# A two-layer decoder trunk in three-product fp32: pairs of hidden blocks from a feed-forward's first block on, the first pair's products in another order, and room handed back sooner

## The chip, the cores and the metric

The kernel runs on one core of a Trainium2 chip. The metric is device microseconds of one execution, the median of several. One row of a profile is one instruction (or a group of like ones) with its start and duration on an engine: PE is the matrix engine, DVE the vector engine, ACT the scalar engine, POOL the GpSimd engine, SP the one that issues most DMAs.

## The reference, cut to what matters

Two layers, each a half-step feed-forward, a mixer (attention and a state-space scan), and a second half-step feed-forward, over 512 tokens of width 1024. The change touches the feed-forwards (FFN) and the hand-over from the mixer to the second one.

```python
def rms_norm(x, gain):
    return x * lax.rsqrt(jnp.mean(x * x, axis=-1, keepdims=True) + NORM_EPS) * gain

def swiglu(h, w_up, w_down):
    gate, up = jnp.split(h @ w_up, 2, axis=-1)          # 1024 -> 2 * 2816
    return (jax.nn.silu(gate) * up) @ w_down            # 2816 -> 1024

for l in range(2):
    x = x + 0.5 * swiglu(rms_norm(x, ffn1_norm[l]), ffn1_w_up[l], ffn1_w_down[l])
    x = x + mixer(rms_norm(x, mix_norm[l])) @ w_out[l]
    x = x + 0.5 * swiglu(rms_norm(x, ffn2_norm[l]), ffn2_w_up[l], ffn2_w_down[l])
return rms_norm(x, final_norm)
```

## The kernel before

Activations lie feature-major: eight tiles `x[m]` of 128 features by 512 tokens. Every product in full precision is three matmuls on rounded operands (`mm3`): high part times high part (L292), high activation times low weight (L293), low activation times high weight (L294). So each activation tile is split into `hhi` (ACT, L477) and `hlo` (DVE, L479), and each weight unit into `whi` (ACT, L259) and `wlo` (DVE, L261).

A weight unit is 128 x 1024 numbers (512 KB): `fetch` issues its load on SP (L219), `convert` splits it, both some units ahead of use. `unit_order` writes the order of all units out; PE uses them in just that order. Everything but the matmuls and the loads runs as small generators, stepped by `tick` while PE's matmuls are written: a `yield n` puts a step n ticks later, and `spawn(g, n)` starts one n ticks late. The instruction order of each engine follows from that; each engine then works through its own queue in order.

An FFN has 22 hidden blocks of 128 in three slices (0-7, 8-15, 16-21); after each slice come eight `down` units, one for each output tile `m`. A hidden block in the ordinary way is a gate unit and an up unit of 24 matmuls over 512 tokens each. Two blocks (j and j+1) can instead be done as a "pair" (`pair_of_blocks`): seven products in the manner of Strassen, in the order of `SEVEN`, with 24 matmuls over 256 tokens each. The products named 11, 12, s2, s1, s3, s4, 22 use four stored weight units and three sums. The weight sums are made here: s1 and s3 by a load on SP (L225) and an accumulating DMA on POOL's queue (L231, in `onto`), s2 = s1 + unit 11 and then s4 = s2 + unit 12 by DVE additions (L244, in `add`). Products 11, 12 and s4 read the split tiles `h`; s2, s1, s3 and 22 read combined inputs `diff`, four pairs of tiles `th` (ACT, L364) and `tl` (DVE, L368), which `combine` makes from `x` (`uv`, L352 to L359) once for each FFN. `combine` starts when an `x` tile is final (from `x_final`), or by fixed delays in the first FFN of layer 0.

Which blocks go as pairs is told by `pairs_from`: in the first FFN of layer 0 blocks 6 to 21, in the other three blocks 2 to 21. The norm's factor `rs` comes late: matmuls run on gain-scaled inputs, and `rs` is multiplied into gate and up (DVE L523; POOL L536; in pairs L599). `FFN (layer, f)` below counts f as 1 and 2. In each FFN but the first, the last steps of the part before it (`down` or `out` units) finish the eight `x` tiles one by one: x (L625 or L1094), `hhi`, `hlo`, the square (`sq`, `acc`, L496) and `combine`.

Of the kernel before, what the change touches and what calls it, by code (L numbers as in the profile page):

```python
# [11 lines left out]
ALU = mybir.AluOpType  # L12
# [4 lines left out]
P = 128  # L17
SEQ = 512
# [15 lines left out]
SEVEN = ("11", "12", "s2", "s1", "s3", "s4", "22")  # L34
STORED = ("11", "12", "s1", "22")
# [105 lines left out]
class Builder:  # L141
# [7 lines left out]
    def __init__(self, ctx, tc, xT, wflat, par, taps, out):  # L149
# [10 lines left out]
        self.sums, self.early, self.summed = {}, {}, 0  # L160
# [53 lines left out]
    def fetch(self, i):  # L214
# [8 lines left out]
        for key in self.early.get(i, ()):  # L223
            raw = self.t(self.sx, [P, KB * P], key[-1], bufs=2)
            self.nc.sync.dma_start(raw, self.stored(key[:-1] + ("s1",)))  # L225
            self.spawn(self.onto(key, raw), 9)
# [20 lines left out]
    def convert(self, i):  # L247
# [7 lines left out]
        elif key[-1] in ("s2", "s4"):  # L255
            raw = self.sums[key[:-1] + ("s2",)]
# [7 lines left out]
    def ahead(self, look=LOOK):  # L264
# [80 lines left out]
    def combine(self, k, gain):  # L345
# [4 lines left out]
        x = self.x[k]  # L350
# [3 lines left out]
        yield 2  # L354
# [5 lines left out]
        yield 1  # L360
        two = []
        for t in (u, v):
            two.append(self.t(self.tp, [P, SEQ], "th", F32R, bufs=KB))
            nc.scalar.copy(two[-1], t)  # L364
            yield 2
        for i, t, hi in zip((k, m), (u, v), two):
# [3 lines left out]
            yield 1  # L370
# [178 lines left out]
    def pair_of_blocks(self, base, fp, two):  # L549
# [5 lines left out]
        lower, upper = self.h[:n], self.h[n:]  # L555
# [47 lines left out]
        product(chain, "11", lower, a, True)  # L603
        nc.scalar.copy(g1, chain)
        product(ps2, "12", upper, a, True)
# [7 lines left out]
        nc.scalar.copy(c, ps3)  # L613
        product(chain, "s3", diff[:n], b, False)
        nc.vector.tensor_tensor(c, chain, c, op=ALU.add)
        self.spawn(normed_up(c))
        product(ps3, "s4", upper, b, False)
        nc.vector.tensor_tensor(g2, g2, ps3, op=ALU.add)
        self.spawn(activate(g2, up2, b))
# [9 lines left out]
    def x_final(self, m, gain):  # L629
        x = self.x[m]  # L630
        yield 1
        if gain is not None:
            yield from self.norm_split(m, gain)
            if self.tp is not None and m >= KB // 2:
                self.spawn(self.combine(m - KB // 2, gain), 2)
# [461 lines left out]
    def mixer(self, layer):  # L1097
# [13 lines left out]
        with ExitStack() as mix:  # L1111
# [6 lines left out]
            gp = enter(tc.tile_pool(name=f"gates{layer}", bufs=2, reuse_waits="tile"))  # L1118
# [42 lines left out]
            with tc.tile_pool(name=f"mg{layer}", bufs=KB, reuse_waits="tile") as mg, \  # L1161
                    tc.tile_pool(name=f"gr{layer}", bufs=2, reuse_waits="tile") as gr:
# [25 lines left out]
                branches.close()  # L1188
                self.open_x()
                self.open_t()  # L1190
                for m in OUT_ORDER:
                    nc.sync.dma_start(self.x[m], xd[m])
                    ps = self.t(self.pmm, [P, SEQ], "mm")
                    self.dense(ps, self.unit(layer, "out", m), self.merged, 0, KB)
                    if m == 0:
                        self.norm_start()
                    self.spawn(self.mix_out(ps, m, gain))
# [164 lines left out]
```

## Time and profile before

| | |
|---|---|
| median of 3 runs | 2616.57 us (2616.45 to 2617.44) |
| profiled execution | 2617.7 us, span 2615.8 us |
| granted PE clock | 0.998 |
| PE busy | 2592.5 us, 99% |
| DVE busy | 1750.1 us, 67% |
| ACT / POOL busy | 1299.0 us, 50% / 508.9 us, 19% |
| chain that ended last | PE 93%, DVE 4%, ACT 1%, DMA 1% |

Where the four FFNs start ordinary blocks and pairs in this execution (us from the span's start): in FFN (0,1) block 4 starts at 52.72 and the first pair at 76.36; FFN (0,2) starts at 961.73 and its first pair at 984.40; FFN (1,1) at 1305.74 and 1330.21; FFN (1,2) at 2256.06 and 2278.73. A busy share is the union of an engine's instruction times over the span. Matmuls overlap in the records, so that their pitch (start to start) and not their duration is what one costs.

### The profile page before, as it was taken

Reading aid. Unit: us, or ns where it says so; the run is one execution under the profiler, and the core shown is the slowest. Engines: PE = TensorE matmul, PEld = TensorE weight load, DVE = VectorE, ACT = ScalarE, POOL = GpSimd, SP = SyncE. Lnnn points to the kernel's source line nnn. Section 1 sums busy time; section 2 is a strip of 40 time slices with the busy share of each in tenths; the row PEclk is TensorE's granted clock in tenths of the full one; section 3 lists DMA queues with packets and bytes.
Section 4 is the critical chain, followed back from the end, with each engine's and each line's share of the span. In section 5 each row is a group of like instructions: output and inputs, shape, how many; then the busy total and the mean of one; then the engine's idle time right before and its main releaser. Section 6 shows DMA issues by size and latency. Waiting matters only on the chain.

```text
span 2615.8 us, 38022 instructions
## 1 busy us (share of the span) xinstructions
PE 2592.5 (99%) x15000; PEld 2289.3 (88%) x15000; DVE 1750.1 (67%) x2352; ACT 1299.0 (50%) x2094; POOL 508.9 (19%) x629
## 2 busy tenths in 40 slices
PE   9999999999999999999999999999999999999997
PEld 7898988888888889899998989888888888899996
DVE  7576876565665478585885858766666744776765
ACT  6343556655554255353553535566555543543444
POOL 1121201133232003021120312012332410121110
PEclk9999999999999999999999999999999999999999
DMA  6555442333323546463554644423333235474642
GB/s 182 141 150 140 122 138 76 104 107 106 114 91 99 163 145 163 136 184 110 159 144 123 179 127 131 130 79 105 98 117 105 97 105 155 138 183 129 177 120 75
DMA packets 102850, 336.35 MB, mean 129 GB/s; under 512 B 12000, under 2 KB 13280, under 8 KB 102672
## 3 DMA queue, kind: packets, MB, share of 16 engines
q1 hardware_dynamic: 91440, 294.00, 35.7%
q0 software_dynamic: 10944, 39.85, 8.7%
q8 instruction: 118, 1.93, 0.3%
q14 instruction: 60, 0.49, 0.1%
q10 hardware_dynamic: 288, 0.07, 0.0%
HBM read 321.20 MB, written 12.68 MB: 128 GB/s over the span
## 4 chain that ended last, share of the span: by engine, by line
PE 93%; DVE 4%; ACT 1%; DMA 1%; issue 1%; POOL 0%; SPq 0%; DVEq 0%; ACTq 0%
PE mm L292 26%; PE mm L294 26%; PE mm L293 26%; PE pa L293 3%; PE pa L294 3%; PE pa L292 3%; PE pa L999 1%; PE pt L762 1%; PE pa L836 1%; DVE wlo L261 1%; PE pa L1001 1%; PE pt L984 1%; PE pt L982 1%; DVE cv L900 0%; ACT whi L259 0%
## 5 line engine op out<-in xcount | busy, mean ns | idle before, releaser
L259 ACT CAST whi<-wraw 128x1024 fp32r<-128x1024 f32 (+2 forms) x434 | 434.2, 1000 | 592.2 <-PE mm L294 504.6
L292 PE MATMUL mm<-hhi,whi 128*128 128x512 f32 (+1 forms) x1856 | 679.5, 366 | 1.1 <-ACT hhi L477 1.1
L293 PE MATMUL mm<-hhi,wlo 128*128 128x512 f32 (+1 forms) x1856 | 658.8, 355 | 2.3 <-DVE wlo L261 2.1
L294 PE MATMUL mm<-hlo,whi 128*128 128x512 f32 (+1 forms) x1856 | 660.4, 356 | 0.1
L261 DVE TENSOR_TENSOR wlo<-wraw,whi 128x1024 fp32r<-128x1024 f32 (+2 forms) x434 | 542.3, 1250 | 168.2 <-ACT whi L259 166.3
L294 PEld LDWEIGHTS mm<-hlo,whi 128*128 128x128 f32 x1856 | 350.9, 189 | 51.7 <-DVE hlo L479 0.5
L293 PEld LDWEIGHTS mm<-hhi,wlo 128*128 128x128 f32 x1856 | 351.7, 190 | 47.1 <-DVE wlo L261 3.5
L292 PEld LDWEIGHTS mm<-hhi,whi 128*128 128x128 f32 x1856 | 351.5, 189 | 44.0 <-ACT hhi L477 1.5
L599 POOL TENSOR_TENSOR g<-g,rs 128x512 f32<-128x512 f32 x76 | 133.2, 1752 | 735.8 <-DVE g L606 715.3
L261 DVE TENSOR_TENSOR wlo<-s,whi 128x1024 fp32r<-128x1024 f32 x152 | 235.5, 1563 | 58.2 <-ACT whi L259 58.2
L292 PE MATMUL mm<-act,whi 128*128 128x512 f32 x704 | 274.0, 389 | 0.0
L293 PE MATMUL mm<-act,wlo 128*128 128x512 f32 x704 | 274.0, 389 | 0.0
L294 PE MATMUL mm<-act,whi 128*128 128x512 f32 x704 | 273.9, 389 | 0.0
L292 PE MATMUL mm<-th,whi 128*128 128x256 f32 x912 | 258.1, 283 | 0.0
L293 PE MATMUL mm<-th,wlo 128*128 128x256 f32 x912 | 258.1, 283 | 0.0
L294 PE MATMUL mm<-tl,whi 128*128 128x256 f32 x912 | 258.1, 283 | 0.0
L259 ACT CAST whi<-s 128x1024 fp32r<-128x1024 f32 x152 | 158.9, 1046 | 100.5 <-PE mm L294 59.0
L625 DVE SCALAR_TENSOR_TENSOR x<-mm,x 128x512 f32<-128x512 f32 x96 | 66.1, 689 | 201.1 <-PE mm L294 201.1
L292 PEld LDWEIGHTS mm<-th,whi 128*128 128x128 f32 x912 | 175.1, 192 | 0.0
L293 PEld LDWEIGHTS mm<-th,wlo 128*128 128x128 f32 x912 | 175.1, 192 | 0.0
L294 PEld LDWEIGHTS mm<-tl,whi 128*128 128x128 f32 x912 | 175.1, 192 | 0.0
L900 DVE SCALAR_TENSOR_TENSOR cv<-mm,conv,cv 128x511 f32<-128x511 f32 (+2 forms) x192 | 142.4, 742 | 24.7 <-ACT cv L897 22.8
(256 smaller groups left out, 4538.7 us busy)
## 6 DMA issues: line engine op xcount, KB each, us to landing
wraw<-in_wflat_dram SPq DMA_DIRECT2D x354, 512.0 KB, 3.7
s<-in_wflat_dram SPq DMA_DIRECT2D x76, 512.0 KB, 5.5
s<-in_wflat_dram POOLq DMA_DIRECT2D x76, 512.0 KB, 9.3
wraw<-in_wflat_dram SPq DMA_DIRECT2D x64, 384.0 KB, 3.1
cumb<-cum_d SPq DMA_DIRECT2D x16, 768.0 KB, 4.0
xd<-x SPq DMA_DIRECT2D x16, 256.0 KB, 3.2
wraw<-in_wflat_dram SPq DMA_DIRECT2D x16, 256.0 KB, 3.2
x<-xd SPq DMA_DIRECT2D x16, 256.0 KB, 5.3
```

The source lines that it names most:

```text
L259: nc.scalar.copy(hi[:, :n], raw[:, :n])
L261: nc.vector.tensor_tensor(lo[:, :n], raw[:, :n], hi[:, :n].bitcast(F32), op=ALU.subtract)
L292: mm(ps, a[0], b[0], start=start, stop=False, **kw)
L293: mm(ps, a[1], b[0], start=False, stop=False, **kw)
L294: mm(ps, a[0], b[1], start=False, stop=stop, **kw)
L599: eng.tensor_tensor(r, r, self.rs[:, cols].unsqueeze(1).to_broadcast([P, 2, half]), op=ALU.mult)
L625: self.nc.vector.scalar_tensor_tensor(x, pd, 0.5, x, op0=ALU.mult, op1=ALU.add)
L762: self.nc.tensor.transpose(pt[:, cs], src[:, cs], self.ident)
L836: nc.tensor.matmul(pz[:, (i - j) * P:n], lhs, part, start=False, stop=(i == j and part is sps[i][1]), skip_group_check=True)
L900: nc.vector.scalar_tensor_tensor(u[:, i:], ps[:, :SEQ - i], tap[KCONV - 1 - i], u[:, i:], op0=ALU.mult, op1=ALU.add)
L982: nc.tensor.matmul(pc[:, :P], bt[:, span(c)], ct[:, span(c)], start=True, stop=True)
L984: nc.tensor.matmul(pu, btok[:, c, :], xws[c].rearrange("p h d -> p (h d)"), start=True, stop=True)
```

## The change

Four pairs take the place of eight ordinary blocks: pairs begin at block 4 in FFN (0,1) and at block 0 in the other three. Since the combined inputs are then wanted at once, the first pair of each FFN runs its products in the order 11, 12, s4, s2, s1, s3, 22 (`FIRST_SEVEN`), where the first three read `h` alone. For that s4 gets a tile and a PSUM bank of its own, and its addition comes before the other's use. The tiles of s1 to s4 move to the pool of the combined inputs, which is open from the mixer on, so the loads of s1 and s3 are no longer held to the FFN's fifth unit: s1 is loaded with the unit two before 11, s3 with 11. `combine` takes other delays. In the mixer the gate tiles go to the side of the branch pools and are closed with them, after the first `out` unit, and the eight loads of `x` are then issued together.

```diff
+FIRST_SEVEN = ("11", "12", "s4", "s2", "s1", "s3", "22")
 def pairs_from(layer, f):
-    return 6 if (layer, f) == (0, 1) else 2
+    return 4 if (layer, f) == (0, 1) else 0
 # unit_order
-                    for part in SEVEN:
+                    for part in (FIRST_SEVEN if j == pairs_from(layer, f) else SEVEN):
 # the weight stream's set-up
-            if key[2:] == ("gate", 0):
-                first = i + 4
-            if "pair" in key and key[-1] in ("s1", "s3"):
-                self.early.setdefault(max(first, i - (5 if key[-1] == "s1" else 4)), []).append(key)
+            if "pair" in key and key[-1] == "11":
+                self.early[i - 2], self.early[i] = key[:-1] + ("s1",), key[:-1] + ("s3",)
 # fetch
-            raw = self.t(self.sx, [P, KB * P], key[-1], bufs=2)
+            raw = self.t(self.tp, [P, KB * P], key[-1], bufs=2)
 # add
-            r = a = self.sums[base + ("s2",)]
-            b = self.sums.pop(base + ("12",))
+            yield 3
+            a, b = self.sums[base + ("s2",)], self.sums.pop(base + ("12",))
+        r = self.sums[key] = self.t(self.tp, [P, KB * P], key[-1], bufs=1)
 # ahead
-            if self.keys[i][-1] in ("s2", "s4"):
-                self.spawn(self.add(self.keys[i]))
+            key = self.keys[i]
+            if key[-1] in ("s2", "s4") and key not in self.adding:
+                for part in (("s2", "s4") if self.keys[i - 1][-1] == "12" and key[-1] == "s4" else key[-1:]):
+                    self.adding.add(key[:-1] + (part,))
+                    self.spawn(self.add(key[:-1] + (part,)))
 # combine
+        x, pause = self.x[k], 1 if m == KB - 1 else 2
...
         two = []
         for t in (u, v):
+            yield pause
             two.append(self.t(self.tp, [P, SEQ], "th", F32R, bufs=KB))
             nc.scalar.copy(two[-1], t)
-            yield 2
+        yield pause
         for i, t, hi in zip((k, m), (u, v), two):
             lo = self.t(self.tp, [P, SEQ], "tl", F32R, bufs=KB)
             nc.vector.tensor_tensor(lo, t, hi.bitcast(F32), op=ALU.subtract)
             self.diff[i] = (hi, lo)
-            yield 1
 # pair_of_blocks
+        first = base[-1] == pairs_from(*base[:2])
+        if first:
+            ps4 = self.t(self.pa, [P, SEQ], "pa")
+            product(ps4, "s4", self.h[n:], b, True)
         product(chain, "s2", diff[n:], b, False)
         nc.scalar.copy(g2, chain)
+        if first:
+            nc.vector.tensor_tensor(g2, g2, ps4, op=ALU.add)
...
 # ffn
-                            self.spawn(self.combine(k, gain), 10 + 9 * k)
+                            self.spawn(self.combine(k, gain), 10 + 8 * k)
 # mixer: the last projection
-                branches.close()
-                self.open_x()
-                self.open_t()
                 for m in OUT_ORDER:
-                    nc.sync.dma_start(self.x[m], xd[m])
                     ps = self.t(self.pmm, [P, SEQ], "mm")
                     self.dense(ps, self.unit(layer, "out", m), self.merged, 0, KB)
                     if m == 0:
+                        branches.close()
+                        self.open_x()
+                        self.open_t()
+                        for r in OUT_ORDER:
+                            nc.sync.dma_start(self.x[r], xd[r])
                         self.norm_start()
-                    self.spawn(self.mix_out(ps, m, gain))
+                    self.spawn(self.mix_out(ps, m, gain), 9 if m == 0 else 0)
```

What this does to the queues is seen at three places. The names in the rows carry instance numbers; `s` is a weight sum, `mm` and `pa` are PSUM banks, `a` and `act` the product silu(gate) * up and its split.

The first place is DVE around block 4 of FFN (0,1). Before, these rows prepare the gate and up units of blocks 4 and 5:

```order
L261 TENSOR_TENSOR wlo_514<-wraw_385,whi_513 128x1024
L368 TENSOR_TENSOR tl_530<-uv_476,th_500 128x512
L368 TENSOR_TENSOR tl_535<-uv_477,th_519 128x512
L355 SCALAR_TENSOR_TENSOR uv_537<-x_89,par_106,uv_537 128x256
L356 TENSOR_TENSOR uv_537<-uv_538,uv_537 128x256
L358 SCALAR_TENSOR_TENSOR uv_538<-uv_537,uv_538 128x256
L359 SCALAR_TENSOR_TENSOR uv_538<-uv_538 128x256
L523 TENSOR_TENSOR g_502<-mm_503,rs_390 128x512
L261 TENSOR_TENSOR wlo_565<-wraw_445,whi_564 128x1024
```

Now the first `wlo` below is that of product 11, the second that of 12, the third that of s4, the fourth that of s2:

```order
L261 TENSOR_TENSOR wlo_515<-wraw_383,whi_514 128x1024
L361 SCALAR_TENSOR_TENSOR uv_521<-uv_520,uv_521 128x256
L362 SCALAR_TENSOR_TENSOR uv_521<-uv_521 128x256
L371 TENSOR_TENSOR tl_554<-uv_520,th_544 128x512
L371 TENSOR_TENSOR tl_556<-uv_521,th_549 128x512
L525 TENSOR_TENSOR g_505<-mm_506,rs_390 128x512
L244 TENSOR_TENSOR s_116_569<-s_57_288,wraw_383 128x1024
L261 TENSOR_TENSOR wlo_567<-wraw_447,whi_566 128x1024
L244 TENSOR_TENSOR s_117_582<-s_116_569,wraw_447 128x1024
L547 TENSOR_TENSOR a_610<-mm_561,g_505 128x512
L387 TENSOR_TENSOR act_380<-a_610,act_379 128x512
L261 TENSOR_TENSOR wlo_613<-s_117_582,whi_612 128x1024
```

Between the first and the second weight split of the place stand now the last two `tl` steps and the addition of s2, and before the third the addition of s4; both are wanted by PE half as long apart as before, since a pair's product has matmuls of half the length.

The second place is POOL's queue at the very start. Before:

```order
L454 AFFINE_SELECT tri<-neg 128x128
L536 TENSOR_TENSOR g_169<-g_169,rs_390 128x512
L536 TENSOR_TENSOR g_285<-g_285,rs_390 128x512
L536 TENSOR_TENSOR g_383<-g_383,rs_390 128x512
L231 DMA s_100_506<-in_wflat_dram 128x1024
L536 TENSOR_TENSOR g_502<-g_502,rs_390 128x512
```

Now:

```order
L456 AFFINE_SELECT tri<-neg 128x128
L231 DMA s_57_288<-in_wflat_dram 128x1024
L538 TENSOR_TENSOR g_166<-g_166,rs_390 128x512
L538 TENSOR_TENSOR g_282<-g_282,rs_390 128x512
L231 DMA s_75_385<-in_wflat_dram 128x1024
L538 TENSOR_TENSOR g_381<-g_381,rs_390 128x512
```

The first accumulating DMA (of s1) moved from behind three multiplications by `rs` to the head of the queue, the second (s3) to behind two of them.

The third place is DVE at the start of FFN (1,1), where the last two `x` tiles (m = 3 and 7) are finished. Before:

```order
L625 SCALAR_TENSOR_TENSOR x_8555<-mm_12238,x_8555 128x512
L358 SCALAR_TENSOR_TENSOR uv_12273<-uv_12272,uv_12273 128x256
L359 SCALAR_TENSOR_TENSOR uv_12273<-uv_12273 128x256
L479 SCALAR_TENSOR_TENSOR hlo_12297<-x_8555,par_107,hhi_12296 128x512
L261 TENSOR_TENSOR wlo_12289<-wraw_12198,whi_12288 128x1024
L496 TENSOR_TENSOR acc_12081<-acc_12081,sq_12305 128x512
L368 TENSOR_TENSOR tl_12345<-uv_12272,th_12302 128x512
L625 SCALAR_TENSOR_TENSOR x_8559<-mm_12279,x_8559 128x512
L368 TENSOR_TENSOR tl_12354<-uv_12273,th_12315 128x512
L479 SCALAR_TENSOR_TENSOR hlo_12357<-x_8559,par_107,hhi_12356 128x512
```

Now:

```order
L636 SCALAR_TENSOR_TENSOR x_8698<-mm_12455,x_8698 128x512
L244 TENSOR_TENSOR s_2093_12504<-s_2041_12287,wraw_12371 128x1024
L361 SCALAR_TENSOR_TENSOR uv_12488<-uv_12487,uv_12488 128x256
L362 SCALAR_TENSOR_TENSOR uv_12488<-uv_12488 128x256
L481 SCALAR_TENSOR_TENSOR hlo_12512<-x_8698,par_107,hhi_12511 128x512
L261 TENSOR_TENSOR wlo_12502<-wraw_12414,whi_12501 128x1024
L498 TENSOR_TENSOR acc_12294<-acc_12294,sq_12518 128x512
L244 TENSOR_TENSOR s_2098_12527<-s_2093_12504,wraw_12414 128x1024
L636 SCALAR_TENSOR_TENSOR x_8702<-mm_12494,x_8702 128x512
L371 TENSOR_TENSOR tl_12568<-uv_12487,th_12524 128x512
L371 TENSOR_TENSOR tl_12570<-uv_12488,th_12535 128x512
L481 SCALAR_TENSOR_TENSOR hlo_12573<-x_8702,par_107,hhi_12572 128x512
```

The additions of s2 and s4 stand now ahead of the low parts of the last two tiles (`hlo`). At the starts of FFN (0,2) and (1,2) they stand in the same way, one ahead of the low part of tile 3 and the other ahead of the last `x`.

More of the change, by code (lines that the diff above doesn't have):

```diff
@@ L222, in fetch @@
         self.raw.append(raw)
[L223 to L224 removed]
+        if i in self.early:
+            key = self.early[i]
+            raw = self.t(self.tp, [P, KB * P], key[-1], bufs=2)
             self.nc.sync.dma_start(raw, self.stored(key[:-1] + ("s1",)))
@@ L255, in convert @@
         elif key[-1] in ("s2", "s4"):
-            raw = self.sums[key[:-1] + ("s2",)]
+            raw = self.sums[key]
         hi = self.t(self.wsp, [P, KB * P], "whi", F32R)
@@ L602, in pair_of_blocks @@
         g1, g2 = (self.t(fp, [P, SEQ], "g", bufs=4) for _ in range(2))
-        product(chain, "11", lower, a, True)
+        product(chain, "11", self.h[:n], a, True)
         nc.scalar.copy(g1, chain)
-        product(ps2, "12", upper, a, True)
+        product(ps2, "12", self.h[n:], a, True)
         nc.vector.tensor_tensor(g1, g1, ps2, op=ALU.add)
         self.spawn(activate(g1, up1, a))
+        first = base[-1] == pairs_from(*base[:2])
+        if first:
+            ps4 = self.t(self.pa, [P, SEQ], "pa")
+            product(ps4, "s4", self.h[n:], b, True)
         assert None not in self.diff
@@ L613, in pair_of_blocks @@
         nc.scalar.copy(c, ps3)
+        if first:
+            nc.vector.tensor_tensor(g2, g2, c, op=ALU.add)
+            self.spawn(activate(g2, up2, b))
         product(chain, "s3", diff[:n], b, False)
@@ L616, in pair_of_blocks @@
         self.spawn(normed_up(c))
-        product(ps3, "s4", upper, b, False)
-        nc.vector.tensor_tensor(g2, g2, ps3, op=ALU.add)
-        self.spawn(activate(g2, up2, b))
+        if not first:
+            product(ps3, "s4", self.h[n:], b, False)
+            nc.vector.tensor_tensor(g2, g2, ps3, op=ALU.add)
+            self.spawn(activate(g2, up2, b))
         product(chain, "22", diff[n:], a, False)
@@ L634, in x_final @@
             if self.tp is not None and m >= KB // 2:
-                self.spawn(self.combine(m - KB // 2, gain), 2)
+                self.spawn(self.combine(m - KB // 2, gain), 1 if m == KB - 1 else 2)
         else:
@@ L1117, in mixer @@
                 tc.tile_pool(name=f"yt{layer}", bufs=24, side="right", reuse_waits="tile"))
-            gp = enter(tc.tile_pool(name=f"gates{layer}", bufs=2, reuse_waits="tile"))
+            gp = branches.enter_context(
+                tc.tile_pool(name=f"gates{layer}", bufs=2, side="right", reuse_waits="tile"))
             gates, self.gated = {}, {}
@@ L1160, in mixer @@
                 self.flush()
-            with tc.tile_pool(name=f"mg{layer}", bufs=KB, reuse_waits="tile") as mg, \
-                    tc.tile_pool(name=f"gr{layer}", bufs=2, reuse_waits="tile") as gr:
+            with tc.tile_pool(name=f"mg{layer}", bufs=KB, reuse_waits="tile") as mg:
+                gr = branches.enter_context(
+                    tc.tile_pool(name=f"gr{layer}", bufs=2, side="right", reuse_waits="tile"))
                 self.merged = []
```

10 lines of the change are left out of this document (3 added, 7 removed).

## The prediction

> **What bounds the kernel now.** I read the engines' busy times first, then the chain that ended last, then the groups with idle time, and last the FFN starts in the windows and in time order. From the page, engines and chain:
>
> ```profile
> PE 2592.5 (99%) x15000; PEld 2289.3 (88%) x15000; DVE 1750.1 (67%) x2352; ACT 1299.0 (50%) x2094; POOL 508.9 (19%) x629
> PE 93%; DVE 4%; ACT 1%; DMA 1%; issue 1%; POOL 0%; SPq 0%; DVEq 0%; ACTq 0%
> L293 PE MATMUL mm<-hhi,wlo 128*128 128x512 f32 (+1 forms) x1856 | 658.8, 355 | 2.3 <-DVE wlo L261 2.1
> ```
>
> PE is the bound, but 67% for DVE is a mean. Of PE's 23.3 us without work (2615.8 less 2592.5) 2.1 us are a wait for `wlo`, so I look where DVE is near full. The busy times by stage (us, then busy us of each engine and its instruction count, clock, DMA share): two ordinary blocks at the start of three FFNs, and a pair behind each:
>
> ```profile
> 52.72:76.36 23.64, 22.06 (x97) 17.94 (x96) 19.59 (x23) 10.32 (x15) 5.06 (x4) 1.00 0.60 149
> 961.73:984.40 22.67, 22.67 (x99) 18.40 (x98) 16.97 (x22) 12.38 (x17) 4.57 (x4) 1.00 0.73 222
> 984.40:1004.55 20.15, 20.15 (x169) 20.14 (x168) 15.65 (x15) 10.45 (x13) 6.40 (x5) 1.00 0.63 162
> 1305.74:1330.21 24.47, 23.35 (x100) 18.17 (x98) 21.37 (x30) 14.55 (x21) 3.00 (x2) 1.00 0.30 93
> 2256.06:2278.73 22.67, 22.67 (x99) 18.40 (x98) 16.98 (x22) 12.37 (x17) 4.57 (x4) 1.00 0.75 220
> ```
>
> The third number after the window's length is DVE's. At the FFN starts it is busy 19.59 of 23.64, 16.97 of 22.67, 21.37 of 24.47: it has 4.0, 5.7 and 3.1 us to spare. These are just the stages that the change fills with pairs. Two of them hold PE's waits already: 1.97 us for `wlo` in block 4 of FFN (0,1) (52.72 to 54.69), 1.46 less a pitch for the last `hhi` in FFN (1,1).
>
> ```profile
> 52.72 0.39 PE L292 MATMUL mm<-hhi,whi 128*128 128x512 f32 x1
> 54.69 0.50 PE L293 MATMUL mm<-hhi,wlo 128*128 128x512 f32 x1 [1.58 <-DVE wlo L261]
> 1311.75 0.50 PE L292 MATMUL mm<-hhi,whi 128*128 128x512 f32 x1 [1.06 <-ACT hhi L477]
> ```
>
> **The change, part by part: the gain.** Matmuls over 512 tokens follow each other at 0.227 us:
>
> ```profile
> 22.62 0.39 PE L294 MATMUL mm<-hlo,whi 128*128 128x512 f32 x1
> 23.53 0.39 PE L292 MATMUL mm<-hhi,whi 128*128 128x512 f32 x1
> ```
>
> (four steps between the two, 0.91/4). Two ordinary blocks are 4 units of 24, 96 x 0.2267 = 21.76 us; the remaining 0.91 of the 22.67 window are the norm's two matmuls, which stay. A pair is 168 matmuls in 20.15 us, 0.120 each. So a pair saves 1.60 us of PE, and four pairs 6.4 us: 2617.7 would become 2611.3.
>
> **What DVE must do for it.** Durations by DVE row, where `wlo` and the addition take 1.22, a 512-wide step 0.68 (pitch 0.61), a 256-wide one 0.42 to 0.48:
>
> ```profile
> 57.61 0.42 DVE L359 SCALAR_TENSOR_TENSOR uv<-uv 128x256 f32<-128x256 f32 x1
> 57.96 0.68 DVE L523 TENSOR_TENSOR g<-mm,rs 128x512 f32<-128x512 f32 x1
> 58.76 1.23 DVE L261 TENSOR_TENSOR wlo<-wraw,whi 128x1024 fp32r<-128x1024 f32 x1
> 59.91 2.41 DVE L368 TENSOR_TENSOR tl<-uv,th 128x512 fp32r<-128x512 f32 x2
> 62.23 0.68 DVE L545 TENSOR_TENSOR a<-mm,g 128x512 f32<-128x512 f32 x1
> 63.60 0.69 DVE L385 TENSOR_TENSOR act<-a,act 128x512 fp32r<-128x512 f32 x1 [0.69 <-ACT act L380]
> 72.08 1.21 DVE L244 TENSOR_TENSOR s<-s,wraw 128x1024 f32<-128x1024 f32 x1
> 73.21 2.31 DVE L261 TENSOR_TENSOR wlo<-wraw,whi 128x1024 fp32r<-128x1024 f32 x1
> ```
>
> Two ordinary blocks take 4 `wlo` (4.9) and 6 steps (4.1), 9.0 us. A pair takes 7 `wlo` (8.5), 2 additions (2.4) and 8 steps (5.5), 16.4 us: 7.4 more, in 1.6 us less time. A budget: 9.0 us of spare DVE time are wanted at each place, and 3.1 to 5.7 are there. If all of it had to fit in the stage with no gap, the stage would last 19.59 + 7.4 = 27.0 (before 23.64), 16.97 + 7.4 = 24.4 (22.67), 21.37 + 7.4 = 28.8 (24.47): +3.4, +1.7 twice, +4.3. The last steps of a pair can run into the next pair, so this is a bound from the dear side; now the order in the queue.
>
> Another lengthening is in these rows. The `wlo` at 73.21 takes 2.31 instead of 1.22, and the two `tl` at 59.91 take 2.41, where two pitches and a rest are 1.29: each time POOL is in a multiplication by `rs`:
>
> ```profile
> 59.87 1.29 POOL L536 TENSOR_TENSOR g<-g,rs 128x512 f32<-128x512 f32 x1 [9.07 <-ACT g L534]
> 72.96 1.48 POOL L536 TENSOR_TENSOR g<-g,rs 128x512 f32<-128x512 f32 x1 [4.64 <-ACT g L534]
> ```
>
> POOL's step ends at 74.44, and `wlo` at 75.52, 1.08 behind it: DVE waits for POOL and then runs at its own speed, about 1.1 us each. [...] By mere sharing of a width, the first `wlo` would lengthen by less, and the terms below would lose 0.5 to 1.1 us each.
>
> *FFN (0,1), block 4.* `wlo` of 11 keeps its place: PE's wait of 1.97 stays. PE wants the `wlo` of 12 one product later, 54.69 + 2.88 = 57.6. Behind `wlo` of 11 (end 54.64) now stand two `uv` (0.92), two `tl` (1.22), a `g` (0.61), the addition of s2 (1.13) and `wlo` itself (1.22): 59.7, or 60.8 when POOL's step falls on it: wait 2.1 to 3.3. Then the addition of s4 (1.13), `a` and its split (1.37 from 62.23 to 63.60, 0.61) and `wlo` (1.22) take 4.3 us against one product, 2.88: wait 1.4 to 1.8. With 20.16 of matmuls the pair ends at 52.72 + 1.97 + 20.16 + (3.5 to 5.1) = 78.4 to 80.0, where 76.36 stood: +2.0 to +3.6, I take +2.9.
>
> *FFN (1,1).* The rows before:
>
> ```profile
> 1305.77 0.68 DVE L625 SCALAR_TENSOR_TENSOR x<-mm,x 128x512 f32<-128x512 f32 x1
> 1307.24 0.75 DVE L479 SCALAR_TENSOR_TENSOR hlo<-x,par,hhi 128x512 fp32r<-128x512 f32 x1
> 1307.91 1.22 DVE L261 TENSOR_TENSOR wlo<-wraw,whi 128x1024 fp32r<-128x1024 f32 x1
> 1309.05 0.68 DVE L496 TENSOR_TENSOR acc<-acc,sq 128x512 f32<-128x512 f32 x1
> 1311.73 0.75 DVE L479 SCALAR_TENSOR_TENSOR hlo<-x,par,hhi 128x512 fp32r<-128x512 f32 x1 [0.20 <-ACT hhi L477]
> ```
>
> DVE goes here from one step to the next. With the addition of s2 ahead of it, `hlo` of tile 3 ends at 1307.99 + 1.13 = 1309.1, or 0.5 sooner where `x` no longer waits its turn; product 11 wants it at its 12th matmul, 1305.74 + 11 x 0.12 = 1307.1: wait 1.4 to 2.0. From there to the end of `hlo` of tile 7: `wlo` 1.13, `acc` 0.6, the addition of s4 1.13, `x` 0.6, two `tl` 1.2, `hlo` 0.75, 5.4 us, against one product of 2.88: wait 2.5 to 2.7. Behind it are squares, `combine`, `wlo` of s2, s1, s3 and the three steps of `rs`; by the same chain 0 to 2.8 us more over the five products left, and I take 2.4, since DVE is full. The stage: 0.91 + 20.15 + 1.7 + 2.6 + 2.4 = 27.8 against 24.47, +3.3 (bounds +0.6 and +4.3, the latter from the budget).
>
> *FFN (0,2) and (1,2).* The part before is spread wider, and tile 7 is just in time:
>
> ```profile
> 962.09 0.68 DVE L1094 SCALAR_TENSOR_TENSOR x<-mm,x 128x512 f32<-128x512 f32 x1
> 963.64 0.75 DVE L479 SCALAR_TENSOR_TENSOR hlo<-x,par,hhi 128x512 fp32r<-128x512 f32 x1 [0.86 <-ACT hhi L477]
> 973.73 0.69 DVE L523 TENSOR_TENSOR g<-mm,rs 128x512 f32<-128x512 f32 x1
> ```
>
> `hlo` moves by two additions, from 964.39 to 966.5 at the latest, wanted at 961.73 + 2.88 + 1.32 = 965.9; `rs` becomes ready some 3.5 us later than 973.73, since three more `wlo` stand ahead. POOL's two multiplications then fall on the last `wlo` of this pair and on the first of the next, 0.5 and 0.5 to 1.1 us each, four in all: 2.9 us of waits against the 1.60 saved, +1.3 each (bounds -1.6, all hidden, and +1.7, the budget).
>
> *The opening.* The accumulating DMA at the head of POOL's queue starts when s1's load lands (issued at 10.28, 6.8 us to landing, 17.1), in the fullest stage for the DMA engines (share 0.97, then 1.01):
>
> ```profile
> 10.28 0.95 SPq L225 DMA_DIRECT2D s<-in_wflat_dram  x2
> ...
> s<-in_wflat_dram SPq DMA_DIRECT2D x4, 512.0 KB, 6.8
> ...
> 13.18 1.41 SPq L219 DMA_DIRECT2D wraw<-in_wflat_dram  x2
> 14.00:18.00 4.00, 4.00 (x18) 3.02 (x17) 2.09 (x3) 2.91 (x5) 0.00 (x0) 1.00 0.97 388
> 18.00:21.00 3.00, 2.89 (x13) 2.36 (x13) 1.41 (x3) 1.50 (x3) 0.00 (x0) 1.00 1.01 362
> q0 software_dynamic: 10944, 39.85, 8.7%
> 20.99 1.05 ACT L259 CAST whi<-wraw 128x1024 fp32r<-128x1024 f32 x1 [0.22 <-DMA wraw<-in_wflat_dram]
> 22.60 0.69 DVE L496 TENSOR_TENSOR acc<-acc,tl 128x512 f32<-128x512 f32 x1 [3.08 <-ACT tl L490]
> 24.48 0.50 PE L293 MATMUL mm<-hhi,wlo 128*128 128x512 f32 x1 [0.57 <-DVE wlo L261]
> ```
>
> 8.7% of 2615.8 us over 76 accumulations is 3.0 us of all engines each. The weight that ACT splits at 20.99 has only just landed, ACT's squares come behind that, DVE's `acc` waits for those, and the `wlo` for which PE waits at 24.48 stands behind `acc`. An accumulation ahead of that load moves the chain by 0 (it queues behind) to 2 us (two thirds of 3.0 overlap it): I take 0.5, nearer to nothing: the load was issued by 14.6 and has landed at 20.99, so that the larger part of it is through before an accumulation issued after 17.1 gets going. [...]
>
> *At nothing.* SP's loads (8 more of sums, 8 fewer of units) stay under the products: DMA share 0.73 at most at these starts. ACT's casts, 7 for 4, are 3.2 us more in stages with 10 us free. The mixer's closing and the loads of `x`, now behind the first `out` unit, stand at the same places in SP's queue; if they came late, it would show as ACT's or DVE's wait for `x` ahead of 961.73.
>
> Sum: the gain of 6.4 is in the stages' sums already; +2.9 + 3.3 + 1.3 + 1.3 + 0.5 = +9.3 us on 2617.7. That execution is 1.1 above the median 2616.57, so 2625.9, say 2626.
>
> **The rivals.** (1) *DVE's lateness all hidden: faster.* The seven products want `wlo` every 2.88 us, and DVE needs 1.13 for it; if `combine` and the norm steps could wait, no product would, and the time were 2616.6 - 6.4 = 2610.2. For it: in the window 984.40 a first pair runs without a wait in DVE time 15.65. Against: there the norm's and `combine`'s work is done before. It decides from 9.0 us of spare DVE time at a start; 3.1 to 5.7 are there.
>
> (2) *The tail goes into the next pair: no change.* The last multiplication by `rs`, `a` twice and `act` twice, some 3 us, run under the second pair, where DVE has 4.5 us left (20.15 less 15.65). Then the budget's stages shrink by 3 us, to 24.0, 21.4 twice and 25.8: +0.4, -1.3, -1.3, +1.3, with the opening's 0.5 about -0.4: 2616 and, if the queue's order costs half of what I count, up to 2621. For it: pairs overlap their tails in steady running. Against: the waits I count are ahead of the tail.
>
> (3) *The opening costs more.* A late `wlo` delays the sum of squares and `rs` and pushes the block-4 chain: +2 in place of 0.5, and 1 us in block 4: 2628.5.
>
> **How the numbers follow.** My forecast 0.50, its own range 2622 to 2632 (terms at their lower values, -1.1 from the execution: 2.0 + 0.6 + 1.3 + 1.3 + 0 = 5.2 gives 2621.8; the upper 3.6 + 4.3 + 1.7 + 1.7 + 2 = 13.3 gives 2629.9, and another POOL step or two 2632). Rival 3: 0.06, rival 2: 0.30, rival 1: 0.14. The range 2612 to 2632 leaves out most of rival 1 and the dear end. About 0.2% (5.2 us) is what a measurement of this kernel can tell from no change: faster is rival 1, 0.14, since 2610.2 lies below 2611.3; same is rival 2 with the few hundredths of my forecast that end below 2621.8, 0.32; the rest, 0.54, is slower.
>
> **What would show it.** In the changed profile, right: PE's L293 idle for `wlo` grows from 2.3 to some 8 us, in the first pair of each FFN, most in (0,1) and (1,1); PE busy falls by 6; DVE near full (over 95%) in these four stages. Wrong: PE's idle time stays at 23 us (rival 1); waits only at the first two products (rival 2); PE idle before 30 us (rival 3). An unforeseen wait, of `out` units for room or of `x` for its loads, would make it wrong outright.

## The result: 25.6 us slower, and where the profile after shows it

The changed kernel takes 2642.56 us (median of 4, 2641.85 to 2648.64) against 2616.93 for the kernel before: ratio 1.0103, 95% interval 1.0086 to 1.0121. The forecast was 2626 (2612 to 2632): the sign was right, the size was not. The profiled execution is the longest of the four, 2648.64 us, with a span of 2646.9; a second profile (below, 2642.2 us) has much the same waits in the first pairs and lacks 3.5 us later in the slices.

Engines, chain and the groups of the page after, as for the kernel before:

```profile
PE 2600.7 (98%) x15288; PEld 2312.1 (87%) x15288; DVE 1766.4 (67%) x2384; ACT 1319.7 (50%) x2118; POOL 497.4 (19%) x641
PE 85%; DVE 8%; ACT 2%; DMA 2%; issue 1%; POOL 0%; DVEq 0%; ACTq 0%; SPq 0%; POOLq 0%
L295 PE MATMUL mm<-hhi,whi 128*128 128x512 f32 (+1 forms) x1792 | 650.1, 363 | 2.4 <-ACT hhi L479 2.4
L296 PE MATMUL mm<-hhi,wlo 128*128 128x512 f32 (+1 forms) x1792 | 630.4, 352 | 7.5 <-DVE wlo L261 7.5
L297 PE MATMUL mm<-hlo,whi 128*128 128x512 f32 (+1 forms) x1792 | 632.1, 353 | 2.2 <-DVE hlo L481 2.2
L295 PE MATMUL mm<-th,whi 128*128 128x256 f32 x1008 | 288.4, 286 | 12.1 <-DVE c L625 12.1
```

PE's idle time has gone from 23.3 to 46.2 us. `wlo` rose from 2.1 to 7.5, near the 8 foreseen, but half of that is luck: 3.8 us are four splits late in the slices, which the second profile lacks (its group holds 5.0), and the rest lies in FFN (0,1) alone and not in the first pair of each FFN. The largest entry, 12.1 us for DVE's `c` (L625), was not foreseen at all. And PE's busy time went up by 8 us where it should have fallen by 6. The stages from the first pair's start to the second pair's start:

```profile
52.44:82.19 29.75, 23.50 (x170) 22.57 (x170) 24.72 (x27) 14.37 (x20) 8.84 (x6) 0.89 0.50 128
967.56:996.39 28.83, 24.39 (x173) 23.30 (x172) 24.93 (x30) 16.11 (x23) 5.76 (x4) 0.89 0.44 124
1319.76:1351.20 31.44, 25.04 (x185) 23.77 (x184) 30.06 (x37) 19.80 (x28) 5.81 (x4) 0.95 0.44 117
2279.16:2307.74 28.58, 23.88 (x172) 22.81 (x171) 24.86 (x30) 16.09 (x22) 5.76 (x4) 0.88 0.46 125
```

A pair's 168 matmuls keep PE busy for 20.15 us, and 21.06 with the norm's two; here it is busy for 23.5 to 25.0, and the granted clock (third number from the end) is 0.88 to 0.95, where every such row before read 1.00. Measured at the first `down` unit behind each first slice, the four FFNs lose 5.8, 6.2, 9.1 and 5.9 us in this execution, and 5.1, 5.0, 8.9 and 5.1 in the second profile.

**The wait for `c`.** FFN (0,2) in time order, PE and DVE:

```profile
986.71 0.28 PE L297 MATMUL mm<-tl,whi 128*128 128x256 f32 x1
990.82 0.56 PE L295 MATMUL mm<-th,whi 128*128 128x256 f32 x1 [3.83 <-DVE c L625]
...
984.58 1.94 DVE L261 TENSOR_TENSOR wlo<-wraw,whi 128x1024 fp32r<-128x1024 f32 x1
986.61 1.60 DVE L622 TENSOR_TENSOR g<-g,c 128x512 f32<-128x512 f32 x1
988.25 0.69 DVE L600 TENSOR_TENSOR g<-g,rs 128x512 f32<-128x512 f32 x1
988.86 1.22 DVE L261 TENSOR_TENSOR wlo<-wraw,whi 128x1024 fp32r<-128x1024 f32 x1
989.99 0.68 DVE L625 TENSOR_TENSOR c<-mm,c 128x512 f32<-128x512 f32 x1
```

The matmul at 986.71 is the last of s3. Product 22 accumulates into the same bank `chain`, so DVE must first read what s3 left there, the `c` at 989.99. In the old order s4, which goes to another bank, stands between the two and covers that read. `FIRST_SEVEN` puts s4 third, so 22 comes straight behind s3, while `c` stands on DVE behind `g` (1.60 against 0.68, with POOL in a multiplication by `rs` from 986.18 to 987.67), a multiplication and a weight split.

**The clock.** The same place by windows (busy PE is the second number): the wait, the 6 us behind it, and the 6 us at the same place before:

```profile
987.00:991.00 4.00, 0.18 (x1) 0.21 (x2) 3.96 (x5) 2.08 (x3) 1.71 (x3) 0.87 0.75 174
991.00:997.00 6.00, 6.00 (x30) 6.00 (x30) 3.64 (x4) 0.64 (x1) 1.95 (x1) 0.52 0.58 146
...
984.00:990.00 6.00, 6.00 (x50) 5.92 (x49) 3.63 (x5) 3.10 (x4) 0.00 (x0) 1.00 0.15 58
```

PE does 30 matmuls in the 6 us behind the wait where it does 50 otherwise, at a granted clock of 0.52. It happens in all four FFNs: behind `c` in (0,2) and (1,2), behind block 4's `wlo` in (0,1), behind the waits for `hlo` and `hhi` in (1,1). In FFN (0,1) that wait and DVE's queue ahead of it look like this, first now, then before:

```profile
55.67 0.58 PE L296 MATMUL mm<-hhi,wlo 128*128 128x256 f32 x1 [2.95 <-DVE wlo L261]
50.77 1.28 DVE L371 TENSOR_TENSOR tl<-uv,th 128x512 fp32r<-128x512 f32 x2
52.67 0.48 DVE L358 SCALAR_TENSOR_TENSOR uv<-x,par,uv 128x256 f32<-128x256 f32 x1 [0.61 <-ACT uv L355]
54.40 1.22 DVE L261 TENSOR_TENSOR wlo<-wraw,whi 128x1024 fp32r<-128x1024 f32 x1
...
52.81 0.69 DVE L385 TENSOR_TENSOR act<-a,act 128x512 fp32r<-128x512 f32 x1 [1.16 <-ACT act L380]
```

### The profile page after: what moved, and what is told of

It is laid out like the page before. It is cut to its first block, busy times and chain, and to the rows that moved or that the text cites. A ratio compares the mean times of both kernels' runs of the same rounds, so it can differ in the third digit from the quotient of the medians.

```text
span 2646.9 us, 38712 instructions
## 1 busy us (share of the span) xinstructions
PE 2600.7 (98%) x15288; PEld 2312.1 (87%) x15288; DVE 1766.4 (67%) x2384; ACT 1319.7 (50%) x2118; POOL 497.4 (19%) x641
## 3 DMA queue, kind: packets, MB, share of 16 engines
q8 instruction: 120, 1.97, 0.3%
## 4 chain that ended last, share of the span: by engine, by line
PE 85%; DVE 8%; ACT 2%; DMA 2%; issue 1%; POOL 0%; DVEq 0%; ACTq 0%; SPq 0%; POOLq 0%
PE mm L295 23%; PE mm L297 23%; PE mm L296 23%; PE pa L296 3%; PE pa L297 3%; PE pa L295 3%; DVE wlo L261 2%; PE pa L1009 1%; PE pt L772 1%; DMA wraw<-in_wflat_dram 1%; ACT whi L259 1%; PE pa L846 1%; PE pa L1011 1%; PE pt L994 1%; DVE s L244 1%
## 5 line engine op out<-in xcount | busy, mean ns | idle before, releaser
L295 PE MATMUL mm<-hhi,whi 128*128 128x512 f32 (+1 forms) x1792 | 650.1, 363 | 2.4 <-ACT hhi L479 2.4
L296 PE MATMUL mm<-hhi,wlo 128*128 128x512 f32 (+1 forms) x1792 | 630.4, 352 | 7.5 <-DVE wlo L261 7.5
L297 PE MATMUL mm<-hlo,whi 128*128 128x512 f32 (+1 forms) x1792 | 632.1, 353 | 2.2 <-DVE hlo L481 2.2
L295 PE MATMUL mm<-th,whi 128*128 128x256 f32 x1008 | 288.4, 286 | 12.1 <-DVE c L625 12.1
L296 PE MATMUL mm<-th,wlo 128*128 128x256 f32 x1008 | 288.3, 286 | 0.0
L297 PE MATMUL mm<-tl,whi 128*128 128x256 f32 x1008 | 287.7, 285 | 0.0
L259 ACT CAST whi<-s 128x1024 fp32r<-128x1024 f32 x168 | 176.1, 1049 | 129.9 <-PE mm L297 64.3
L295 PEld LDWEIGHTS mm<-th,whi 128*128 128x128 f32 x1008 | 196.0, 194 | 12.8 <-ACT whi L259 11.5
L296 PEld LDWEIGHTS mm<-th,wlo 128*128 128x128 f32 x1008 | 196.1, 195 | 0.7 <-DVE wlo L261 0.6
L297 PEld LDWEIGHTS mm<-tl,whi 128*128 128x128 f32 x1008 | 195.9, 194 | 0.0
```

Of the source, the lines that this page charges most:

```text
L259: nc.scalar.copy(hi[:, :n], raw[:, :n])
L295: mm(ps, a[0], b[0], start=start, stop=False, **kw)
L296: mm(ps, a[1], b[0], start=False, stop=False, **kw)
L297: mm(ps, a[0], b[1], start=False, stop=stop, **kw)
```

## The experiments

**The changed kernel again** (no edit).

> The changed kernel once more, unaltered, for a second profile and as the yardstick of this set. The profile at hand (2648.6 us) is 6 us above the other executions (2642.4). If these 6 us are the four waits for a weight split late in some slices (0.5 to 2.0 us each, 3.9 in all), a second profile shows them smaller or gone and lies near 2642.5; if they belong to the change, they are there again. Median expected: 2642.

Measured: 2642.3 (2641.01 to 2642.76). The four late weight splits of the first profile are gone; the 12.1 us for `c` are there again (1.08, 3.86, 3.06, 4.10). The 6 us were not the change's in every execution.

**Extra matmuls in the wait.**

```diff
+        if first and base[1] == 2:
+            pt = self.t(self.ptr, [P, SEQ], "pt")
+            for i in range(28):
+                nc.tensor.matmul(pt[:, a], diff[0][0][:, :P], diff[0][0][:, a], start=i == 0, stop=i == 27)
         product(chain, "22", diff[n:], a, False)
```

> The changed kernel with 28 extra matmuls of 256 tokens ahead of the last product (22) of the first pair in FFN (0,2) and (1,2); their result is used by nothing. PE waits there 3.8 and 4.1 us for DVE's c, and runs at a granted clock of 0.50 for some 6 us behind it, 27 matmuls at 0.213 in place of 0.120. Theory (the drop of the clock follows from PE's idleness): the extra work takes 3.4 us of the wait and nothing more, the clock stays at 1.00, 2 x 2.5 us less: about 2637.5. Rival (the slow matmuls come from the accumulating DMA or from DVE and POOL at their ports): no change, 2642.5, and the pitch behind the wait stays 0.213.

Measured: 2639.6 (2638.95 to 2641.81), 2.7 us less than the unaltered run beside it. FFN (0,2), PE in time order and the window behind it:

```profile
987.69 3.52 PE L634 MATMUL pt<-th 128*128 128x256 f32 x28
991.73 0.36 PE L295 MATMUL mm<-th,whi 128*128 128x256 f32 x1 [0.52 <-DVE c L625]
...
991.00:997.00 6.00, 5.48 (x46) 5.31 (x46) 5.71 (x6) 2.53 (x4) 2.19 (x1) 1.00 0.68 167
```

The clock stays at 1.00 (0.52 in the first profile without these matmuls) with the DMA share at 0.68 and POOL busy for 2.19 us of the 6, against 0.58 and 1.95 there: here it is the idleness of PE that brings the drop. The rival falls. The gain is half of what I expected, since the drops at these two places cost 1.56 and 1.51 us in the second profile (17 and 16 slow matmuls), and not the 2.5 of 27 matmuls that I had taken from FFN (0,2) in the first. The stages of these two FFNs lose 3.6 and 3.7 us here where the second profile has 5.0 and 5.1.

**Old starts, all the rest of the change.**

```diff
-    return 4 if (layer, f) == (0, 1) else 0
+    return 6 if (layer, f) == (0, 1) else 2
```

> The changed kernel with the pairs beginning where they began before (block 6 in FFN (0,1), block 2 elsewhere); all other parts of the change are in it: order of the first pair, the tiles of s1 to s4, the loads, the delays, the mixer's hand-over. Theory (the loss comes from the first pairs' places, where the norm and combine work is): near the kernel before, 2616 to 2619. Rival (the moved loads and tiles cost by themselves: the loads of s1 and s3 now stand next to each other ahead of the unit loads in SP's queue in all pairs): 3 to 8 us above it, spread over the slices.

Measured: 2627.7 (2626.71 to 2630.76), 10.8 us above the kernel before: my theory of the moment was wrong, and by more than the rival allowed. The four added pairs themselves cost 14.6 of the 25.5; the rest of the change, which I had not costed, cost 10.8. The trace shows `c` waited for 1.08 us in each of the four first pairs, 2.86 for block 4's `wlo`, and (this execution is the longest of the four) a late unit load at 1504, in the loads of SP and the casts of ACT:

```profile
1489.17 3.39 SPq L225 DMA_DIRECT2D s<-in_wflat_dram  x2
1493.36 10.34 SPq L218 DMA_DIRECT2D wraw<-in_wflat_dram  x3
...
1504.57 1.05 ACT L259 CAST whi<-wraw 128x1024 fp32r<-128x1024 f32 x1 [5.79 <-DMA wraw<-in_wflat_dram]
```

The kernel before, a pair's loads:

```profile
1356.43 0.33 SPq L225 DMA_DIRECT2D s<-in_wflat_dram  x1
1358.17 0.33 SPq L219 DMA_DIRECT2D wraw<-in_wflat_dram  x1
1360.40 0.33 SPq L225 DMA_DIRECT2D s<-in_wflat_dram  x1
1364.90 6.06 SPq L219 DMA_DIRECT2D wraw<-in_wflat_dram  x2
```

In the pairs behind the first ones too, the loads of s1 and s3 and with them both accumulating DMAs now go ahead of the unit loads. The next three runs take that, the product order and the delays away, one after the other.

**Without the hold of s4's addition** (the `yield 3` in `add`; old starts).

```diff
-            yield 3
             a, b = self.sums[base + ("s2",)], self.sums.pop(base + ("12",))
```

> The kernel with the old starts of the pairs and all other parts of the change, but s4's addition not held back by three ticks. With that hold the unit loaded for product 12 is free later, and in SP's queue the loads of s1 and s3 come one behind the other ahead of the unit loads; without it they alternate with them as before the change. Theory (late unit loads behind two accumulating DMAs cost 2 to 5 us over the steady pairs): 2627.7 falls to 2624 to 2625, and no wait for the split of product 12 is left in the steady pairs. Rival (the loads land in time anyway, the 10.8 us over the kernel before lie only in the first pairs and block 4): 2627.5.

Measured: 2623.7 (2621.93 to 2624.23), 4.0 us less. The loads alternate again (`s`, `wraw`, `s`, `wraw` twice), and no steady pair waits:

```profile
1485.58 0.33 SPq L225 DMA_DIRECT2D s<-in_wflat_dram  x1
1487.32 0.33 SPq L218 DMA_DIRECT2D wraw<-in_wflat_dram  x1
1489.55 0.33 SPq L225 DMA_DIRECT2D s<-in_wflat_dram  x1
1494.05 6.06 SPq L218 DMA_DIRECT2D wraw<-in_wflat_dram  x2
```

**The old product order as well.**

```diff
-        first = base[-1] == pairs_from(*base[:2])
+        first = False
-FIRST_SEVEN = ("11", "12", "s4", "s2", "s1", "s3", "22")
+FIRST_SEVEN = SEVEN
```

> The same, and the first pairs run their products in the old order too (s4 between s3 and 22). Theory (22 straight behind s3 costs PE a wait of 1.24 us a pair even where the norm is long done): 4 x 1.24 = 5.0 us less than the run without the hold, about 2619.5. Rival (DVE's wait only moves to the next product): no change.

Measured: 2618.7 (2617.02 to 2620.14), 5.0 us less, just the four waits of 1.24 (1.08 of each are idle in the records); the trace has no wait for `c` left.

**The old delays of `combine` as well** (its old body, and 10 + 9k).

> The same, and combine takes its old delays (10 + 9k, and its old yields). What is left of the change are the tiles of s1 to s4, the mixer's pools and loads. Theory (the new delays put DVE's uv and tl steps of combine ahead of block 4's weight split in FFN (0,1): PE waits 2.9 us instead of 1.6, and then runs for some 5 us at half clock, together 3.7 us): 2616.9, as before the change. Rival (the moved tiles and the mixer's hand-over cost as well): 2618 or more.

Measured: 2617.3 (2616.39 to 2617.88), ratio to the kernel before 1.0001 (0.9992 to 1.0010). Block 4's `wlo`, the group over all of the kernel: 3.4 us of waits with the new delays, 2.4 with the old ones.

```profile
L295 PE MATMUL mm<-hhi,wlo 128*128 128x512 f32 (+1 forms) x1856 | 659.5, 355 | 3.5 <-DVE wlo L260 3.4
...
L295 PE MATMUL mm<-hhi,wlo 128*128 128x512 f32 (+1 forms) x1856 | 658.8, 355 | 2.4 <-DVE wlo L260 2.4
```

By the medians the delays cost 1.4, less than the 3.7 expected: the trace before this step shows only 6 slow matmuls of 512 (1.2 us), and FFN (1,1) was 0.8 us better with the new delays. Three of the eleven executions before this step (2617.0) lie among those behind it, eight lie above them all (2618.6 to 2620.1); whether the half clock at block 4 divides them is not shown, since one alone was profiled. What is left, the moved tiles and the mixer's hand-over, costs nothing that can be measured. So the 10.8 split into 4.0 + 5.0 + 1.4 + 0.4.

**s1 between s3 and 22** (all four new starts).

```diff
+FIRST_SEVEN = ("11", "12", "s4", "s2", "s3", "s1", "22")
+        if first:
+            product(chain, "s3", diff[:n], b, False)
+            nc.scalar.copy(c, chain)
+            product(ps3, "s1", diff[:n], a, True)
+            nc.vector.tensor_tensor(g2, g2, ps3, op=ALU.add)
+            self.spawn(activate(g2, up2, b))
+            nc.vector.tensor_tensor(c, c, ps3, op=ALU.add)
...
```

> The changed kernel with the first pair's products in the order 11, 12, s4, s2, s3, s1, 22: s1, which goes to its own bank, stands between s3 and 22, and ACT copies the shared bank after s3; nothing is left out. Theory (22 waits for DVE to read what s3 left, because no product stands between them any more; 12.1 us in the four first pairs, and two drops of the clock of 2.5 us behind it): these waits go, about 0.7 us a pair come for ACT's copy between s2 and s3: 2642.5 - 12 - 5 + 3 = about 2628.5. Rival (DVE's sum of work is the bound in the stage, and a wait that is taken away comes back at the next product): within 4 us of 2642.5.

Measured: 2635.0 (2634.54 to 2638.64), 7.3 us less; the theory's 14 were too many, but it is well beyond the rival's 4. The wait for `c` is gone entirely, ACT's copy between s2 and s3 is there at 0.68 us a pair, and the splits behind are later:

```profile
L295 PE MATMUL mm<-th,whi 128*128 128x256 f32 x1008 | 285.6, 283 | 2.7 <-ACT g L615 2.7
L296 PE MATMUL mm<-th,wlo 128*128 128x256 f32 x1008 | 286.6, 284 | 1.8 <-DVE wlo L261 1.8
L296 PE MATMUL mm<-hhi,wlo 128*128 128x512 f32 (+1 forms) x1792 | 629.4, 351 | 10.0 <-DVE wlo L261 10.0
...
2314.13 1.05 ACT L259 CAST whi<-wraw 128x1024 fp32r<-128x1024 f32 x1 [5.22 <-DMA wraw<-in_wflat_dram]
2317.70 0.39 PE L296 MATMUL mm<-hhi,wlo 128*128 128x256 f32 x1 [1.15 <-DVE wlo L261]
```

12.1 us went and 2.7 + 1.8 came in the first two groups. The third holds 10.0 us against 5.0 in the second profile of the changed kernel: waits of 1.15, 1.33 and 0.93 us in FFN (1,2), each for a unit load that landed late, as in the run with the old starts (this profile is of the longest execution, 2638.64). So the rest came back in part through late loads; that DVE, full in the stage, takes back some as well, as the rival has it, fits the 1.8 but was not separated.

**Without the additions.** In the first pairs s2 and s4 read s1's weights, so that this kernel leaves part of the layer's work out.

```diff
+        if key[3] == pairs_from(*key[:2]):
+            self.sums[key] = a
+            return
         r = self.sums[key] = self.t(self.tp, [P, KB * P], key[-1], bufs=1)
```

> The changed kernel without the two DVE additions of the first pair in each FFN: products s2 and s4 read s1's weights there, so their result is not the layer's. Eight additions, 9.8 us of DVE, are gone, nothing else. Theory of the prediction (the additions stand ahead of the low parts and splits that PE wants, and what is late on DVE is late on PE): the waits for hhi and hlo in FFN (1,1) fall from 3.4 us to about 1.5, those of 0.6 in FFN (0,2) and (1,2) go, in (0,1) the waits for the splits of 12 and s4 fall by 1.1 each, the wait for c by up to 2 and half clock behind them in part: about 2629. Rival (they fill gaps of DVE; POOL's multiplications, the norm's chain on ACT and the order of products set the waits): 2638 to 2642.

Measured: 2634.9 (2632.98 to 2637.58), 7.4 us less, between theory and rival. The waits, changed kernel first (FFN (1,1), tile 3 and tile 7), then without additions:

```profile
1322.57 0.39 PE L297 MATMUL mm<-hlo,whi 128*128 128x256 f32 x1 [1.33 <-DVE hlo L481]
1327.20 0.39 PE L295 MATMUL mm<-hhi,whi 128*128 128x256 f32 x1 [1.74 <-ACT hhi L479]
...
1314.21 0.39 PE L300 MATMUL mm<-hlo,whi 128*128 128x256 f32 x1 [0.29 <-DVE hlo L484]
1317.30 0.39 PE L298 MATMUL mm<-hhi,whi 128*128 128x256 f32 x1 [0.20 <-ACT hhi L482]
1318.41 0.39 PE L300 MATMUL mm<-hlo,whi 128*128 128x256 f32 x1 [0.60 <-DVE hlo L484]
...
L298 PE MATMUL mm<-th,whi 128*128 128x256 f32 x1008 | 288.0, 286 | 12.1 <-DVE c L628 12.1
```

So the additions make most of the waits for these parts, as predicted: 3.35 us of idleness with them (0.28 more for the `hlo` of tile 7), 1.09 without. The wait for `c` does not care: 12.1 us with them and without them. It comes from the order.

**All of the mending, four new starts** (s1 between s3 and 22, and the hold in first pairs only).

> Nothing is left out. The changed kernel with all four starts, with s1 between s3 and 22 and the hold of s4's addition in first pairs only. Theory (the terms add): 2635.0 less 4.0 = 2631. Rival (the hold's 4 us were there only because first pairs came late): 2635.

Measured: 2630.9 (2629.62 to 2631.40); the terms add. The group of waits for `wlo` that held 10.0 us holds 5.2 now, and no split is late behind the first slices. By stage it loses 6.2, 1.8, 3.0 and 1.9 us.

**Two new starts only,** FFN (0,2) and (1,2), with the mended order; old starts, old product order elsewhere, old delays in FFN (0,1).

> Nothing is left out. Pairs from block 0 in FFN (0,2) and (1,2) alone, there with s1 between s3 and 22; the old starts and the old product order in FFN (0,1) and (1,1); s4's addition held back only in those first pairs; combine with the old delays in FFN (0,1), the new ones elsewhere. By the terms measured so far each of the two pairs saves 1.6 us and pays hhi and hlo 0.6, ACT's copy between s2 and s3 0.83, and 0.8 for splits behind: about +0.7 each; FFN (1,1) gains 0.8 by the new delays: about 2617.5 to 2618.5, not to be told from the kernel before. Rival (DVE full at the start costs more than these rows show): 2621 or more.

Measured: 2620.0 (2618.99 to 2621.35), ratio 1.0011 (1.0002 to 1.0020): not better than the kernel before. Each new pair loses 1.7 us net here in place of 0.7. No version of these runs beats the kernel before.

## Why the prediction was wrong

- **Right: the gain is 1.60 us a pair at most and DVE is too full at the starts for it.** The budget (3.1 to 5.7 us to spare, 9.0 wanted) gave the sign in all four places. That DVE's work counts, the run without the additions shows (9.8 us of DVE less, 7.4 us of time less). With the two unforeseen terms mended, the stages of FFN (0,2), (1,1) and (1,2) lose 1.8, 3.0 and 1.9 where 1.3, 3.3 and 1.3 were forecast, but (0,1) loses 6.2 where 2.9 was. That the three lie so near is partly luck: in (0,2) and (1,2) the waits are for `hhi` and `hlo`, for ACT's copy, which only the mended order needs, and for two splits of the second pair, where the forecast had POOL's steps alone.
- **Failed step: the new order was read for what the additions delay, and never for which bank each product writes and who must read it first.** "s4 between s3 and 22" is a cover that the change removes; it was not in the list of things costed at nothing either. It is worth 5.0 us where the norm is long done (4 x 1.24), and 12.1 us of waits where it is not; mending it in the changed kernel brought 7.3 net.
- **Failed step: "SP's loads stay under the products".** The DMA share at the starts was the wrong row. The loads of s1 and s3 moved ahead of the unit loads in nearly all pairs, because the addition of s4, and with it the unit of product 12, is held three ticks longer; worth 4.0 us with the old starts and 4.1 between the two mended runs with the new ones. Where it costs differs from execution to execution: the second profile of the changed kernel has no late split behind the first slices.
- **Failed step: "`wlo` of 11 keeps its place", PE's wait of 1.97 stays.** It became 3.23 (2.95 idle). The new delays put two `tl` and two `uv` steps ahead of it, of which DVE's former wait of 1.16 there took up only a part. Between the runs with the new and the old delays it is 1.4 us by the medians.
- **Missing term: the half clock behind a long wait.** No wait in the kernel before had more than 1.58 us of idleness, and its granted clock was 1.00 from 10 to 2600 us. In the second profile it takes 1.5 to 2.5 us at each of four places behind the first FFN: one in (0,2), two in (1,1), one in (1,2). Over all of that profile it is some 90 matmuls of 256 tokens at 0.213 in place of 0.120, by estimate 8.4 us of PE; three of these places follow the wait for `c` and go with it. In FFN (0,1) it costs less than it seems: there the 2.3 us of slow matmuls give DVE time for the split of 12, whose wait came out at 0.70 (1.56 in the second profile) in place of 2.1 to 3.3.
- **Wrong in kind:** POOL's steps on the last splits of FFN (0,2) and (1,2), 2.9 us of waits forecast; in the first pairs there the rows show none for a split, only 0.6 for `hhi` and `hlo`, and instead the `g` in front of `c` takes 1.60 us ((0,2)) and 1.59 ((1,2)) in place of 0.68, while POOL is in its step. The 0.6 follows from the prediction's own two times (`hlo` at 966.5, wanted at 965.9) and was left out of its sum. The opening was put at 0.5 and cost nothing that shows: block 4 starts at 52.44, before at 52.72.
- **Near in size:** the split of s4 in FFN (0,1), 1.52 (1.4 to 1.8 forecast); `hlo` of tile 3 in FFN (1,1), 1.33 (1.4 to 2.0); tile 7 there, 1.74 + 0.28, somewhat less than forecast (2.5 to 2.7).
- **Slips in the working that change nothing here:** there are 4 fewer unit loads (350 for 354) and not 8; `hlo` at 964.39 and two additions of 1.13 are 966.65 and not 966.5; and the lower sum of the range takes +1.3 for FFN (0,2) and (1,2), whose own lower bound was -1.6.

The forecast's 9.3 us thus met 25.5: of the 16 between them the order explains 7.3 and the hold 4.1, both by runs. Of the remaining 4.8, 3.3 lie in FFN (0,1) (6.2 for 2.9). I put them down to the delays there, the half clock left there (23 slow matmuls in the last-but-one run) and the copies that the mended order needs; how they share it was not separated.

## What to carry to other kernels

When a change reorders products that accumulate into one PSUM bank with reads in between, write down for each neighbouring pair who must read the bank and what PE does meanwhile; a product on another bank in between was worth the whole read here (5.0 us over four pairs with the old starts), and the read's place in its engine's queue decided the size (PE idle for 1.08 us in FFN (0,1), 3.83 in (0,2)). A late release of one buffer turned the order of a DMA queue in the pairs behind the first ones too (4.0 us with the old starts), not just where the change is meant to act: compare the queue's order in the steady part too. Replacing matmul time by vector-engine time did not pay here, where the vector engine had 3.1 to 5.7 us to spare at a start and 9.0 were wanted: look for that time in the very stage.

## What the runs showed of the hardware

In the first profile of the changed kernel PE ran at a granted clock of 0.50 (0.213 us for 256 tokens in place of 0.120) behind idle times of 2.95 us (FFN (0,1)), 3.83 ((0,2)) and 4.09 ((1,2)), for some 5 to 6 us each:

```profile
55.67:61.50 5.83, 5.49 (x24) 5.19 (x24) 5.66 (x7) 2.20 (x3) 1.53 (x1) 0.50 0.17 33
990.82:996.80 5.98, 5.98 (x28) 5.98 (x29) 3.62 (x3) 0.44 (x1) 2.13 (x1) 0.50 0.63 154
2302.62:2307.50 4.88, 4.88 (x23) 4.88 (x24) 3.21 (x2) 0.00 (x0) 2.13 (x1) 0.50 0.83 203
```

Shorter waits stood ahead of the half clock too. The changed kernel in FFN (1,1): behind two waits of 1.33 and 1.74 us, and behind one of 1.96:

```profile
1327.90:1331.20 3.30, 3.22 (x15) 3.22 (x16) 3.13 (x7) 2.78 (x5) 0.00 (x0) 0.50 0.12 50
...
1395.00:1400.00 5.00, 4.96 (x29) 4.96 (x30) 4.66 (x6) 2.98 (x5) 0.00 (x0) 0.66 0.00 0
```

With the old starts 1.72 us of idleness stood ahead of it once (PE busy for 0.42 of the 2.00 us from 1506.00 and for 3.86 of the 4.00 behind them, these at a clock of 0.58). Around waits of 1.52 us (changed kernel, 65.00 to 68.00) and 1.58 us (kernel before, 50.00 to 60.00) the clock was 1.00.

The length of a wait does not decide this alone. Here is the wait of 3.05 us in the first profile of the changed kernel, the stretch behind it, and then the stretch behind the same wait (3.06 us, as told above) in the second:

```profile
1342.00:1347.00 5.00, 1.95 (x17) 1.77 (x16) 4.88 (x6) 2.92 (x4) 2.70 (x3) 1.00 0.70 138
1347.00:1352.00 5.00, 5.00 (x44) 5.00 (x43) 4.71 (x5) 2.09 (x3) 1.81 (x1) 1.00 0.70 179
...
1343.90:1347.50 3.60, 3.60 (x18) 3.60 (x18) 2.88 (x2) 0.00 (x0) 1.80 (x1) 0.50 0.96 241
```

In the first the clock stays at 1.00; in the second it is 0.50, which by estimate costs 1.7 us more (18 matmuls at 0.213 in place of 0.120). What decides between the two was not shown. With 28 matmuls in the wait of FFN (0,2) the drop did not come (1.00 from 991.00 to 997.00).
